# Two-layer diffusion backbone: modulation blocks of layer 2 moved to another stretch, FFN value groups regrouped, operand sums moved

## The chip, the cores and the metric

One core of a Trainium2 chip runs the whole program. The metric is the device time of one execution in microseconds; the time given for a kernel is the median of its runs.

## The reference

Two layers work on 512 latent tokens and 256 context tokens of width 1024. Each layer has a token mixer of four branches, merged by gates, and a SwiGLU FFN of hidden width 2816. Both are modulated: a row vector per token kind (`c` for latents, `c_ctx` for the context) is made by one dense product with `w_ada[l]` and cut into six parts, a shift, a scale and a residual gate for the mixer and the same three for the FFN.

```python
mod_x = silu_c @ w_ada[l] + b_ada[l]        # sh_m, sc_m, g_m, sh_f, sc_f, g_f
mod_c = silu_cc @ w_ada[l] + b_ada[l]
hx = modulate(rms_norm(x, norm_mix[l]), sh_m, sc_m)
...
x = x + g_m * mixer_stream(px, ...)         # gates * branches, summed, @ w_out
if not last:
    ctx = ctx + cg_m * mixer_stream(pc, ...)
    ctx = ctx + cg_f * swiglu(modulate(rms_norm(ctx, norm_ffn), csh_f, csc_f), w1, w3, w2)
x = x + g_f * swiglu(modulate(rms_norm(x, norm_ffn), sh_f, sc_f), w1, w3, w2)
return rms_norm(x, final_norm)

def swiglu(h, w1, w3, w2):
    return (silu(h @ w1) * (h @ w3)) @ w2
```

In layer 2 the context is needed for keys and values only, so there only the shift and scale of its mixer are needed: the second and third 2048 columns of `w_ada[1]` matter for the latent row alone.

## The kernel before, in words

Tokens lie along the free axis, channels along the partitions, 128 at a time. Every fp32 matrix product is made of three matmuls, with both operands split into a high and a low part (`mm3`, L526 to L528; `mm3u`, L610 to L612, in the mixer's dense part; `prod`, L1654 to L1659, in the FFN of layer 1). Weights are split on the way: SP issues the load (L231), ScalarE casts the high part `wh` (L221), VectorE subtracts it to get the low part `wl` (L223), with three raw buffers and four each for high and low parts; `Stream` does the same in the dense part (L560, L566, L573).

The layer loop starts at L622. A layer has the mixer, then the *dense stretch* of gates and branch projections, then `w_out` (L1570 and on) with its residual, the norm, and the FFN. `dense` (L1484) runs gate units. Each yield of a unit feeds the weight stream, and every second one (`AJ`) calls a step of the *modulation generator*, from the third unit on.

That generator is `ada_steps` (L112). It makes 2048 columns of `w_ada` (block b of 0, 1, 2) in four quarters of eight steps. A step has a load of 256 KB on SP (L120), and on VectorE, for each row, one multiply (L133) or multiply-add (L131) of 128x512. At the end of a quarter TensorE transposes the accumulator in four pieces (L145) and VectorE reduces them (L146). `live` says how many rows (token kinds) each block has. An `issue_after` makes all its VectorE work wait for the last low part of the norm issued before (`lastn`, L182). Block 0 has shift and scale of the mixer, block 1 the mixer's residual gate and the FFN's shift, block 2 the FFN's scale and its gate. For layer 1, blocks 1 and 2 are made in layer 1's dense stretch. For layer 2 all three are made during layer 1's FFN (L1583), through `ada_next`: `NAF` steps behind each pass of FFN blocks, `NAN` steps behind each weight load of a down projection.

The FFN of layer 1 has 22 blocks of 128 hidden channels (`groups`), each group first up (`ffn_up` or `ffn_pair`), then down through `w_ffn2` (loop at L1794), with the result added to the residual stream by `resid` (L1565). `ffn_up` (L1594) makes a block from its weights directly, for given token ranges: `oh` is 0 to 512 and 512 to 768, `halves` is 0 to 384 and 384 to 768. `ffn_pair` makes two blocks at once by `quad` (L1661), a Strassen-like scheme with seven products of half size. It needs sums of weights (made by POOL, split as above) and sums of activations T1 to T4, which `prepare` (L1611) makes once, by POOL, VectorE and ScalarE; T1 overwrites a part of `h`. In the first group the first four blocks (`NCV`) go by ranges, while `norm_range` (L184) of the second range runs: a step of it per block, with squares and statistics, POOL's power, the broadcast transposes (L202), and for each of eight chunks a product (L208), an affine and a cast on ScalarE (L178, L181) and the low part (L182). In the last group the down projection goes range by range, and the norm for layer 2 follows each range.

In layer 2 the FFN has no pairs, and deeper weight buffers of its own pool `gp` (three extra `wh` and `wl`, eight `ws`), which lie where the mixer's pools were. Before it, `mg`, the merged branches, is split (L1557, L1558).

The order of the instructions on each engine is planned ahead of the run: a planner goes through the program and gives each engine, of what it holds to be ready, what stands first in the program. So work that stands later fills gaps, and a stall at run time is not replanned.

Of the kernel before, what the change touches and what calls it, by code (L numbers as in the profile page):

```python
# [43 lines left out]
NAN = 5  # L44
NCV = 4
# [18 lines left out]
def block_kernel(ctx: ExitStack, tc: tile.TileContext, x, c, ctx_in, c_ctx, w_ada, b_ada, norm_mix, w_in,  # L64
# [557 lines left out]
    for l in range(DEPTH):  # L622
# [10 lines left out]
        with ExitStack() if l else first as st:  # L633
# [836 lines left out]
            if l == 0:  # L1470
                ab = []

                def three():
                    flat = sbank().rearrange("p a b -> p (a b)")
                    return [flat[:, i * 512:(i + 1) * 512] for i in range(3)]

                def abufs():
                    if not ab:
                        ab.extend(utile(512, "wada") for _ in range(5))
                    return ab[:2], ab[2:]  # L1480

                ada = [ada_steps(0, b, three, abufs) for b in (1, 2)]
# [21 lines left out]
        with ExitStack() as st:  # L1504
# [76 lines left out]
            if not last:  # L1581
                wb = [gp.tile([P, 512], F32, tag="wada", name="wada", bufs=4) for _ in range(4)]
                ada = [ada_steps(1, b, lambda: [pf.tile([P, 512], F32, tag="ada", name="pa")],  # L1583
                                 lambda: (wb[:2], wb[2:]), (2, 1, 1)) for b in range(3)]
# [26 lines left out]
            def prepare():  # L1611
                def flat(t):
                    return t.rearrange("p (k n) -> p k n", k=4)

                def blk(i, kb, half):
                    return h[:, i, 4 * kb:4 * kb + 4, HT * half:HT * (half + 1)]

                def put(dst, v):
                    nc.scalar.copy(dst[:, 0], v)
                    nc.vector.tensor_sub(dst[:, 1], v, dst[:, 0])  # L1620

                def scratch():
                    return gp.tile([P, 4, HT], F32, tag="ga", name="sc", bufs=6)

                t3, t2, t4 = [gp.tile([P, 2, 4, HT], F32R, tag="tb", name="tb", bufs=3) for _ in range(3)]
                v, u = scratch(), scratch()
                nc.gpsimd.tensor_sub(u, blk(1, 1, 1), blk(1, 0, 1))
                nc.vector.tensor_sub(v, blk(0, 1, 1), blk(0, 0, 1))
                nc.vector.tensor_add(v, v, u)
                put(t3, v)  # L1630
                v2 = scratch()
                nc.gpsimd.tensor_add(v2, v, blk(1, 0, 0))
                nc.vector.tensor_add(v2, v2, blk(0, 0, 0))
                put(t2, v2)
                u4 = scratch()
                nc.gpsimd.tensor_sub(u4, blk(1, 1, 0), v2)
                nc.vector.tensor_add(u4, u4, blk(0, 1, 0))
                put(t4, u4)
                nc.gpsimd.tensor_sub(v2, blk(1, 1, 1), v2)
                nc.vector.tensor_add(v2, v2, blk(0, 1, 1))  # L1640
                t1 = h[:, :, 0:4, HT:2 * HT]
                put(t1, v2)
                tops.update(T1=t1, T2=t2, T3=t3, T4=t4, B11=h[:, :, 0:4, 0:HT], B21=h[:, :, 4:8, 0:HT],
                            B22=h[:, :, 4:8, HT:2 * HT])

# [112 lines left out]
            if fast:  # L1758
                groups = [list(range(0, 6)), list(range(6, 12)), list(range(12, 18)), list(range(18, 22))]
            for gi, grp_ in enumerate(groups):  # L1760
# [6 lines left out]
                elif gi == 0:  # L1767
                    todo = [(grp_[:NCV], [r]) for r in oh]
                elif fast:
                    todo = []  # L1770
                for fs, rngs in todo:
# [8 lines left out]
                    if f:  # L1780
                        ada_next(NAF)
                if fast:
                    if gi == 0:
                        prepare()
                    for f in grp_[NCV if gi == 0 else 0::2]:
# [8 lines left out]
                for rngs in ([[r] for r in oh] if lastg else [halves]):  # L1794
                    for n in range(NC_):
# [3 lines left out]
                        ada_next(NAN)  # L1799
# [70 lines left out]
```

## Time and profile before

| | |
|---|---|
| median of 3 runs | 2665.15 us (2663.88 to 2666.01) |
| the profiled execution's own time | 2665.27 us |
| its span, first to last instruction | 2663.3 us |
| TensorE busy | 2548.0 us (96%), mean granted clock 0.985 |
| VectorE busy | 1852.1 us (70%) |
| ScalarE busy | 1171.7 us (44%) |
| GpSimd busy | 237.2 us (9%) |

PE is TensorE, DVE is VectorE, ACT is ScalarE, POOL is GpSimd, SP issues most loads. A matmul's busy time covers the whole time that it is in the pipeline, so matmuls overlap, and a busy share near 100% can hide a slow stream: the number of matmuls in a window tells more. A row of the groups reads: line, engine, operation, output<-inputs, shapes, count | busy us, mean ns of one | idle before, and what ended it.

### The profile page before, as it was taken

To read this page: it belongs to the slowest core of one execution; us is meant where nothing else is said; L and a number is where in the kernel's file an instruction comes from. 1 tells how busy PE (TensorE), PEld (TensorE's weight loads), DVE (VectorE), ACT (ScalarE), POOL (GpSimd) and SP (SyncE) were. 2 spreads that over 40 slices of the span, in tenths; PEclk is the share of its full clock that TensorE was granted. 3 is DMA by queue.
4 is the path that set the end of the run, shared out by engine and by line. 5 is a ranking of instruction groups with operands and counts; after the bars stand their busy time and mean duration, and the time that the engine had idled before them with its cause. 6 is when DMAs were issued, how large, how long until landed. Compare 5 with 4: busy or idle time off the path is not lost.

```text
span 2663.3 us, 38749 instructions
## 1 busy us (share of the span) xinstructions
PE 2548.0 (96%) x14435; PEld 2328.1 (87%) x14435; DVE 1852.1 (70%) x3205; ACT 1171.7 (44%) x2324; POOL 237.2 (9%) x255
## 2 busy tenths in 40 slices
PE   7999999999999998898999999999999999999998
PEld 5999889999999987898999978788888888988888
DVE  5967887786878668888675579887766635733335
ACT  5245555556422354323232354566665423722235
POOL 2000000000000011223030310100000000000000
PEclk9999999999999999999999999999999999999999
DMA  8211112222245354354442243111222235633333
GB/s 289 69 40 44 44 33 72 60 62 66 90 141 168 112 172 116 95 158 136 146 119 60 68 133 92 52 44 52 64 78 73 73 96 157 177 98 95 96 95 111
DMA packets 400800, 262.53 MB, mean 99 GB/s; under 512 B 15946, under 2 KB 368532, under 8 KB 400612
## 3 DMA queue, kind: packets, MB, share of 16 engines
q1 hardware_dynamic: 393332, 236.14, 30.0%
q0 software_dynamic: 7280, 23.93, 3.2%
q8 instruction: 113, 1.85, 0.3%
q14 instruction: 75, 0.61, 0.1%
HBM read 243.23 MB, written 8.91 MB: 95 GB/s over the span
## 4 chain that ended last, share of the span: by engine, by line
PE 80%; DVE 8%; issue 4%; DMA 4%; ACT 3%; SPq 0%; POOL 0%; DVEq 0%; POOLq 0%; ACTq 0%
PE pf L610 10%; PE pf L611 10%; PE pf L612 10%; PE pf L528 10%; PE pf L527 10%; PE pf L526 10%; PE pf L1658 8%; PE pS L907 3%; PE pT L936 2%; DMA wada<-in_w_ada_dram 2%; PE pv L1346 2%; PE pv L1435 1%; DVE wl L223 1%; DVE wada L131 1%; DMA ws<-in_w_in_dram 1%
## 5 line engine op out<-in xcount | busy, mean ns | idle before, releaser
L221 ACT CAST wh<-ws 128x512 fp32r<-128x512 f32 (+2 forms) x407 | 242.2, 600 | 531.1 <-PE pf L527 370.4
L610 PE MATMUL pf<-h,wh 128*128 128x384 f32 (+1 forms) x1280 | 459.4, 359 | 1.9 <-ACT tg L782 1.3
L612 PE MATMUL pf<-h,wl 128*128 128x384 f32 (+1 forms) x1280 | 448.7, 351 | 0.0
L611 PE MATMUL pf<-h,wh 128*128 128x384 f32 (+1 forms) x1280 | 447.8, 350 | 0.0
L223 DVE TENSOR_TENSOR wl<-ws,wh 128x512 fp32r<-128x512 f32 (+2 forms) x407 | 277.1, 686 | 186.9 <-ACT wh L221 183.0
L528 PE MATMUL pf<-h,wl 128*128 128x512 f32 (+2 forms) x784 | 279.1, 359 | 8.2 <-DVE wl L223 8.2
L526 PE MATMUL pf<-h,wh 128*128 128x512 f32 (+2 forms) x784 | 277.1, 360 | 8.8 <-ACT h L181 5.3
L527 PE MATMUL pf<-h,wh 128*128 128x512 f32 (+2 forms) x784 | 279.3, 359 | 1.0 <-DVE h L182 0.9
L566 ACT CAST wh<-ws 128x512 fp32r<-128x512 f32 x264 | 164.1, 623 | 235.3 <-PE pf L611 197.5
L610 PEld LDWEIGHTS pf<-h,wh 128*128 128x128 f32 x1280 | 241.6, 189 | 16.3 <-ACT tg L782 2.0
L611 PEld LDWEIGHTS pf<-h,wh 128*128 128x128 f32 x1280 | 241.8, 189 | 13.4 <-issue 0.6
L612 PEld LDWEIGHTS pf<-h,wl 128*128 128x128 f32 x1280 | 241.0, 188 | 13.3 <-issue 0.2
L573 DVE TENSOR_TENSOR wl<-ws,wh 128x512 fp32r<-128x512 f32 x264 | 181.1, 687 | 96.8 <-ACT wh L566 95.6
L704 DVE SCALAR_TENSOR_TENSOR ca<-ub,cols,ca 128x798 f32<-128x798 f32 (+1 forms) x240 | 215.3, 897 | 4.0
L131 DVE SCALAR_TENSOR_TENSOR wada<-wada,sil 128x512 f32<-128x512 f32 x224 | 183.6, 840 | 30.5 <-DMA wada<-in_w_ada_dram 28.9
L527 PE MATMUL pf<-g,wh 128*128 128x384 f32 (+2 forms) x584 | 197.4, 339 | 0.0
L528 PE MATMUL pf<-g,wl 128*128 128x384 f32 (+2 forms) x584 | 196.1, 339 | 0.0
L526 PE MATMUL pf<-g,wh 128*128 128x384 f32 (+2 forms) x584 | 195.8, 340 | 0.0
L526 PEld LDWEIGHTS pf<-h,wh 128*128 128x128 f32 x784 | 148.3, 192 | 31.5 <-ACT h L181 7.9
L528 PEld LDWEIGHTS pf<-h,wl 128*128 128x128 f32 x784 | 150.2, 192 | 29.4 <-DVE wl L223 10.0
L527 PEld LDWEIGHTS pf<-h,wh 128*128 128x128 f32 x784 | 150.1, 192 | 23.5 <-DVE h L182 4.2
L938 ACT CAST pt<-pT 128x512 fp32r<-128x512 f32 (+1 forms) x216 | 91.8, 471 | 153.9 <-PE pT L936 153.4
(385 smaller groups left out, 5127.7 us busy)
## 6 DMA issues: line engine op xcount, KB each, us to landing
ws<-in_w_in_dram SPq DMA_DIRECT2D x248, 256.0 KB, 2.9
ws<-in_w_ffn_dram SPq DMA_DIRECT2D x243, 256.0 KB, 2.9
wada<-in_w_ada_dram SPq DMA_DIRECT2D x160, 256.0 KB, 3.0
ws<-in_w_out_dram SPq DMA_DIRECT2D x58, 256.0 KB, 3.1
sq<-in_w_ffn_dram SPq DMA_DIRECT2D x45, 256.0 KB, 4.2
wada<-in_w_ada_dram SPq DMA_DIRECT2D x16, 512.0 KB, 6.8
khl<-khl POOLq DMA_DIRECT2D x40, 192.0 KB, 3.1
ws<-in_w_ffn_dram SPq DMA_DIRECT2D x24, 192.0 KB
```

The costliest lines, as they stand in the source:

```text
L131: nc.vector.scalar_tensor_tensor(accs[r], w, s, accs[r], op0=ALU.mult, op1=ALU.add)
L221: nc.scalar.copy(wh[:, :n], st[:, :n])
L223: lastv[0] = nc.vector.tensor_sub(wl[:, :n], st[:, :n], wh[:, :n]).ins
L526: nc.tensor.matmul(o, lhsT=wh, rhs=xh(k), start=(k == 0), stop=False)
L527: nc.tensor.matmul(o, lhsT=wh, rhs=xl(k), start=False, stop=False)
L528: nc.tensor.matmul(o, lhsT=wl, rhs=xh(k), start=False, stop=(k == n - 1))
L573: nc.vector.tensor_sub(wl, u.raw[i], u.wh[i])
L610: nc.tensor.matmul(o, lhsT=wh, rhs=xh(k), start=(k == 0), stop=False)
L611: nc.tensor.matmul(o, lhsT=wh, rhs=xl(k), start=False, stop=False)
L612: nc.tensor.matmul(o, lhsT=wl, rhs=xh(k), start=False, stop=(k == nk - 1))
L704: nc.vector.scalar_tensor_tensor(a, u, w, a, op0=ALU.mult, op1=ALU.add)
L1658: nc.tensor.matmul(o, lhsT=wt_, rhs=T[:, x_, k], start=(start and k == 0 and i == 0), stop=(stop and k == 3 and i == 2), skip_group_check= ...
```

## The change

Blocks 1 and 2 of layer 2's modulation are made in layer 2's own dense stretch, with one row each; block 0 stays in layer 1's FFN, but its steps come in down projections of the second group on. The groups of layer 1's FFN become 4, 6, 6, 6 in place of 6, 6, 6, 4. In the first group, blocks 0 and 1 go by ranges and blocks 2 and 3 by halves with one load; the pair (4, 5) goes to the second group, so there are still nine pairs. `prepare` becomes a generator of eight steps on half the columns each, one step per output block of the first down projection.

```diff
@@ -41,8 +41,7 @@
 NTS = (2, 2)
 AJ = 2
 NAF = 3
-NAN = 5
-NCV = 4
+NAN = 4
 NAQ = 0
 NSL = 4
 WB = (0, 3)
@@ -1467,7 +1466,7 @@
                 fill.flush()
             conv_split(3, 4)
             ada = []
-            if l == 0:
+            if True:
                 ab = []
 
                 def three():
@@ -1479,7 +1478,7 @@
                         ab.extend(utile(512, "wada") for _ in range(5))
                     return ab[:2], ab[2:]
 
-                ada = [ada_steps(0, b, three, abufs) for b in (1, 2)]
+                ada = [ada_steps(l, b, three, abufs, (1, 1, 1) if last else (2, 2, 2)) for b in (1, 2)]
 
             def dense(units, skip=0):
                 for i, u in enumerate(units):
@@ -1581,7 +1580,7 @@
             if not last:
                 wb = [gp.tile([P, 512], F32, tag="wada", name="wada", bufs=4) for _ in range(4)]
                 ada = [ada_steps(1, b, lambda: [pf.tile([P, 512], F32, tag="ada", name="pa")],
-                                 lambda: (wb[:2], wb[2:]), (2, 1, 1)) for b in range(3)]
+                                 lambda: (wb[:2], wb[2:])) for b in range(1)]
 
             def ada_next(n):
                 for _ in range(n):
@@ -1609,39 +1608,37 @@
             tops = {}
 
             def prepare():
-                def flat(t):
-                    return t.rearrange("p (k n) -> p k n", k=4)
-
-                def blk(i, kb, half):
-                    return h[:, i, 4 * kb:4 * kb + 4, HT * half:HT * (half + 1)]
-
-                def put(dst, v):
-                    nc.scalar.copy(dst[:, 0], v)
-                    nc.vector.tensor_sub(dst[:, 1], v, dst[:, 0])
-
-                def scratch():
-                    return gp.tile([P, 4, HT], F32, tag="ga", name="sc", bufs=6)
-
                 t3, t2, t4 = [gp.tile([P, 2, 4, HT], F32R, tag="tb", name="tb", bufs=3) for _ in range(3)]
-                v, u = scratch(), scratch()
-                nc.gpsimd.tensor_sub(u, blk(1, 1, 1), blk(1, 0, 1))
-                nc.vector.tensor_sub(v, blk(0, 1, 1), blk(0, 0, 1))
-                nc.vector.tensor_add(v, v, u)
-                put(t3, v)
-                v2 = scratch()
-                nc.gpsimd.tensor_add(v2, v, blk(1, 0, 0))
-                nc.vector.tensor_add(v2, v2, blk(0, 0, 0))
-                put(t2, v2)
-                u4 = scratch()
-                nc.gpsimd.tensor_sub(u4, blk(1, 1, 0), v2)
-                nc.vector.tensor_add(u4, u4, blk(0, 1, 0))
-                put(t4, u4)
-                nc.gpsimd.tensor_sub(v2, blk(1, 1, 1), v2)
-                nc.vector.tensor_add(v2, v2, blk(0, 1, 1))
                 t1 = h[:, :, 0:4, HT:2 * HT]
-                put(t1, v2)
                 tops.update(T1=t1, T2=t2, T3=t3, T4=t4, B11=h[:, :, 0:4, 0:HT], B21=h[:, :, 4:8, 0:HT],
                             B22=h[:, :, 4:8, HT:2 * HT])
+                for k in (0, 2):
+                    def blk(i, kb, half):
+                        return h[:, i, 4 * kb + k:4 * kb + k + 2, HT * half:HT * (half + 1)]
+
+                    def put(dst, v):
+                        nc.scalar.copy(dst[:, 0, k:k + 2], v)
+                        nc.vector.tensor_sub(dst[:, 1, k:k + 2], v, dst[:, 0, k:k + 2])
+
+                    u, v = [gp.tile([P, NTOK], F32, tag="ts", name="ts", bufs=2).rearrange("p (k n) -> p k n", k=2)
+                            for _ in range(2)]
+                    nc.gpsimd.tensor_sub(u, blk(1, 1, 1), blk(1, 0, 1))
+                    nc.vector.tensor_sub(v, blk(0, 1, 1), blk(0, 0, 1))
+                    nc.vector.tensor_add(v, v, u)
+                    put(t3, v)
+                    yield
+                    nc.gpsimd.tensor_add(u, v, blk(1, 0, 0))
+                    nc.vector.tensor_add(u, u, blk(0, 0, 0))
+                    put(t2, u)
+                    yield
+                    nc.gpsimd.tensor_sub(v, blk(1, 1, 0), u)
+                    nc.vector.tensor_add(v, v, blk(0, 1, 0))
+                    put(t4, v)
+                    yield
+                    nc.gpsimd.tensor_sub(u, blk(1, 1, 1), u)
+                    nc.vector.tensor_add(u, u, blk(0, 1, 1))
+                    put(t1, u)
+                    yield
 
             def sqtile(name):
                 sqn[0] += 1
@@ -1756,7 +1753,7 @@
 
             groups = [list(range(0, 8)), list(range(8, 15)), list(range(15, 22))]
             if fast:
-                groups = [list(range(0, 6)), list(range(6, 12)), list(range(12, 18)), list(range(18, 22))]
+                groups = [list(range(0, 4)), list(range(4, 10)), list(range(10, 16)), list(range(16, 22))]
             for gi, grp_ in enumerate(groups):
                 gt = []
                 for f in grp_:
@@ -1765,7 +1762,7 @@
                 if gi == 0 and last:
                     todo = [(grp_[:NSL], [r]) for r in oh] + todo[NSL:]
                 elif gi == 0:
-                    todo = [(grp_[:NCV], [r]) for r in oh]
+                    todo = [(grp_[:2], [r]) for r in oh] + todo[2:]
                 elif fast:
                     todo = []
                 for fs, rngs in todo:
@@ -1777,12 +1774,9 @@
                         ffn_up(f, gt[f - grp_[0]], rngs)
                         next(nr, None)
                     drain(nr)
-                    if f:
-                        ada_next(NAF)
-                if fast:
-                    if gi == 0:
-                        prepare()
-                    for f in grp_[NCV if gi == 0 else 0::2]:
+                prep = prepare() if fast and gi == 0 else iter(())
+                if fast and gi:
+                    for f in grp_[::2]:
                         ffn_pair(f, gt[f - grp_[0]], gt[f + 1 - grp_[0]])
                 lastg = gi == len(groups) - 1
                 if lastg:
@@ -1796,7 +1790,9 @@
                         if n in (1, 3, 5, 7):
                             next(fin, None)
                         ws = wload(w_ffn2[l], grp_[0] * P, n * P, len(grp_))
-                        ada_next(NAN)
+                        next(prep, None)
+                        if gi or not fast:
+                            ada_next(NAN)
                         for lo, hi in rngs:
                             pu = gbank()[:, :hi - lo]
                             mm3(pu, ws, lambda k: gt[k][:, 0, lo:hi], lambda k: gt[k][:, 1, lo:hi])
```

## Rows read from the trace of the kernel before

**Rows 1.** The page, the chain that ended last, by engine.

```profile
PE 80%; DVE 8%; issue 4%; DMA 4%; ACT 3%; SPq 0%; POOL 0%; DVEq 0%; POOLq 0%; ACTq 0%
```

**Rows 2.** Unbroken matmul streams, windows: us, busy (count) by engine, clock, DMA.

```profile
1440.00:1460.00 20.00, 20.00 (x116) 20.00 (x115) 9.07 (x20) 3.88 (x8) 0.00 (x0) 1.00 0.20 60
...
2240.00:2260.00 20.00, 20.00 (x171) 20.00 (x170) 11.84 (x22) 7.87 (x14) 0.00 (x0) 1.00 0.68 178
```

**Rows 3.** The same view, layer 1's FFN.

```profile
1034.50:1100.00 65.50, 48.34 (x268) 43.93 (x267) 63.52 (x71) 22.64 (x37) 20.77 (x7) 0.84 0.44 128
1160.00:1280.00 120.00, 107.36 (x585) 103.57 (x584) 101.99 (x152) 37.74 (x66) 41.01 (x27) 0.96 0.49 151
1280.00:1380.00 100.00, 96.29 (x540) 94.43 (x539) 71.76 (x120) 27.69 (x49) 17.89 (x12) 0.98 0.46 136
```

**Rows 4.** The same windows, records of L1658 (one) and of L145 (two) alone.

```profile
1034.50:1100.00 65.50, 16.27 (x66) 14.42 (x67) 0.84 0.44 128
...
1160.00:1280.00 120.00, 3.98 (x24) 2.97 (x24) 0.96 0.49 151
1280.00:1380.00 100.00, 2.40 (x16) 2.00 (x16) 0.98 0.46 136
```

**Rows 5.** TensorE's waits, 1160 to 1380 us.

```profile
PE pf L1658 <- DVE u L1692: 6.9, 3, 3.3
PE pf L1658 <- DVE wl L223: 5.0, 4, 2.2
```

**Rows 6.** VectorE's groups, 1034.5 to 1100 us: busy us, mean ns.

```profile
L131 DVE SCALAR_TENSOR_TENSOR wada<-wada,sil 128x512 f32<-128x512 f32 x22 | 24.9, 1148 | 1.2 <-DMA wada<-in_w_ada_dram 1.1
...
L1628 DVE TENSOR_TENSOR sc<-h 128x1536 f32<-128x1536 f32 x1 | 1.8, 1752 | 0.0
```

**Rows 7.** Timeline of POOL and of VectorE; columns: start us, us, instruction.

```profile
1060.19 3.46 POOL L1636 TENSOR_TENSOR sc<-h,sc 128x1536 f32<-128x1536 f32 x1 [7.86 <-DVE sc L1633]
...
1060.27 3.93 DVE L223 TENSOR_TENSOR wl<-ws,wh 128x512 fp32r<-128x512 f32 x1
```

**Rows 8.** Timeline of TensorE and VectorE around the second range's norm.

```profile
1012.66 0.38 PE L202 MATMUL pT<-ident,r 128*128 128x128 f32 x2
...
1025.25 0.42 DVE L182 TENSOR_TENSOR h<-hn,h 128x256 fp32r<-128x256 f32 x1
1025.59 4.13 DVE L133 TENSOR_SCALAR wada<-wada,sil 128x512 f32<-128x512 f32 x2
```

**Rows 9.** VectorE's groups, first down projection, 1110 to 1160 us.

```profile
L223 DVE TENSOR_TENSOR wl<-ws,wh 128x512 fp32r<-128x512 f32 x8 | 5.5, 689 | 0.7 <-ACT wh L221 0.7
L1565 DVE SCALAR_TENSOR_TENSOR xT<-pf,mod,xT 128x384 f32<-128x384 f32 x6 | 3.7, 612 | 4.9 <-PE pf L528 4.9
...
L1565 DVE SCALAR_TENSOR_TENSOR xT<-pf,mod,xT 128x256 f32<-128x256 f32 x6 | 2.8, 474 | 0.0
...
L1565 DVE SCALAR_TENSOR_TENSOR xT<-pf,mod,xT 128x128 f32<-128x128 f32 x6 | 2.1, 344 | 0.0
...
L1723 DVE TENSOR_TENSOR g<-ts,g 128x768 fp32r<-128x768 f32 x2 | 1.8, 954 | 0.9 <-ACT g L1722 0.9
```

**Rows 10.** Timeline of TensorE, first matmul of layer 2's projections.

```profile
1578.46 0.80 PE L526 MATMUL pf<-h,wh 128*128 128x512 f32 x1 [5.30 <-ACT h L181]
```

**Rows 11.** Layer 1's dense stretch: its window, VectorE's L131 in it, modulation reductions.

```profile
745.00:905.00 160.00, 160.00 (x940) 159.42 (x939) 127.51 (x217) 33.93 (x62) 0.00 (x0) 1.00 0.49 147
...
L131 DVE SCALAR_TENSOR_TENSOR wada<-wada,sil 128x512 f32<-128x512 f32 x96 | 69.0, 746 | 5.5 <-DMA wada<-in_w_ada_dram 4.3 <-DVE wada L131 0.4
...
L146 DVE TENSOR_REDUCE mod<-pS x8: 680/686/692, 829.3 to 892.3; 128x4 f32<-128x512 f32 x8
```

**Rows 12.** Window of layer 2's dense stretch.

```profile
2093.00:2225.00 132.00, 131.69 (x593) 108.05 (x591) 54.96 (x87) 39.01 (x69) 1.38 (x1) 1.00 0.30 86
```

**Rows 13.** Timeline of TensorE, start of layer 2's output projection.

```profile
2231.25 0.58 PE L526 MATMUL pf<-mg,wh 128*128 128x256 f32 x1 [6.21 <-ACT wh L221]
```

**Rows 14.** Layer 1's FFN, multiply-adds with one row, 1278 to 1293 us.

```profile
L131 DVE SCALAR_TENSOR_TENSOR wada<-wada,sil x7: 744/751/754, 1278.6 to 1290.5; 128x512 f32<-128x512 f32 x7
```

## What the change was predicted to do

> **What bounds the kernel now.** First the chain of waits: four fifths of it is TensorE, VectorE has 8%, ScalarE 3% [rows 1]. So the time is the matmuls, which the change leaves alone, plus the stretches in which TensorE does less than it can. What it can do is read from windows in which it never stops: 116 matmuls of 384 columns in 20 us, 0.1724 us each, and 171 of 256 columns, 0.117 us each [rows 2]. Next the windows of layer 1's FFN, with VectorE's column beside TensorE's [rows 3]; the records of pairs (L1658) and of modulation transposes (L145) give the shapes [rows 4].
>
> - 1034.5 to 1100 us (second-range pass of the first four blocks, the sums for the pairs, start of pair (4,5)): 66 records of 384 columns and 202 narrow ones need 66 x 0.1724 + 202 x 0.117 = 35.0 us; the window has 65.5, so 30.5 are lost. VectorE is busy 63.5 of 65.5, and the mean granted clock is 0.84, part of it at the 1.2 GHz level: that cost is inside the 30.5.
> - 1160 to 1280 us (second group's pairs): 561 x 0.1724 + 24 x 0.117 = 99.5; 20.5 lost, VectorE 102 of 120.
> - 1280 to 1380 us: 524 x 0.1724 + 16 x 0.117 = 92.2; 7.8 lost, VectorE 72 of 100.
>
> Together 58.8 us. The waits say who is late: matmuls of pairs wait for VectorE's sums (L1692, 6.9 us) and low weight parts (L223, 5.0 us) [rows 5]. What crowds VectorE is the modulation of layer 2: its multiply-adds (L131) take 22 slots in the first window, of 1.148 us on average [rows 6]; the same instruction takes 0.746 undisturbed [rows 11].
>
> **The change, part by part.** Sums are made against the profiled execution, 2665.3 us (span 2663.3 and 2 around it); it lies 0.1 us from the median. A measurement can tell about 0.2%, 5.3 us, from no change.
>
> *What goes from layer 1's FFN.* Modulation blocks b=1 and b=2 leave (64 multiply steps with one row each, 64 loads on SP's queue, 8 x 4 transposes); b=0 stays with 64 steps (two rows) and is placed in the down projections of the later groups alone. The four wide preparation steps leave the crowded window. I remove the whole 58.8 us and charge the new stretches one by one. What is late next is then the norm of the second range.
>
> *(a) The norm of the second range.* Its broadcast (L202) runs at 1012.66, right behind the second block of the first pass (the code takes one step of the norm per block), and the last low part of h starts at 1025.25, taking 0.42 us [rows 8]: 13.0 us, covered today by blocks 2 and 3. After the change the first pass holds two blocks, so TensorE has nothing wide left. Only block 0's 48 narrow matmuls of the second pass (48 x 0.117 = 5.6 us) can be done chunk by chunk meanwhile; later weights wait for the four weight buffers. 13.0 - 5.6: **+7.4** (0 if the norm is taken earlier, 11 if little interleaves).
>
> *(b) Second pass and blocks 2, 3.* VectorE has some 9 us of gating and low weight parts against the last 5.6 us of narrow matmuls, then wide work: **+4** (0 to 8).
>
> *(c) First down projection, now with the preparation.* TensorE: 8 x 2 x 12 x 0.1724 = 33 us. VectorE: the sums. A 1536-wide one took 1.75 us [rows 6], a 768-wide subtraction 0.95 [rows 9]: 18 half-size ones x 0.95 = 17; 8 low weight parts x 0.69 = 5.5; residuals 8 x (0.612 + 0.474 + 0.344) = 11.4 [rows 9]. That is 34. To this comes blocking: while POOL worked 3.46 us on the sum at 1060.19, a low part (L223) issued at 1060.27 took 3.93 us instead of 0.69 [rows 7]; four such pairs stand in the trace, about 3.2 us each, 12.6 in all. Halves halve each POOL instruction and double their number, so again 12.6: 46 against 33. But about 11 us of the preparation is ready while blocks 2 and 3 still fill TensorE. **+3** (0 to 15).
> The Trainium skill (SBUF — State Buffer, Who interferes with whom and SBUF: two separate sides) calls the port pair of the two engines an exclusive lock that the first holds for its whole instruction. The row of 3.93 us agrees. By the rule alone, every POOL instruction here would block VectorE; that is rival C.
>
> *(d) First pairs and the rest of b=0.* Half of the modulation stays in the FFN, now 64 steps x 0.746 = 48 us spread over two down projections and their neighbours; those have room (7.8 lost even in the third window with it). **+5** (0 to 20, the upper end being the 20.5 of the second window). So the FFN gives -58.8 + 19.4 = -39.4.
>
> *(e) Boundary to layer 2.* The last group has six blocks instead of four, so each range pass is 8 x 18 matmuls of 256 columns (16.8 us) instead of 8 x 12 (11.2). The norm that makes TensorE idle 5.3 us before 1578.46 [rows 10] gets 5.6 us more cover. It also gets 16 more loads, casts and low parts of 256 columns in front of it. **-3.5** (-5.6 to +2). The eight loads saved in the first group offset those on SP's queue.
>
> *(f) Layer 2's dense stretch.* 64 steps and loads come in. Layer 1's dense stretch carries twice the steps: 160 us of TensorE in a 160 us window with VectorE at 127.5 [rows 11]. Layer 2's has VectorE at 55 of 132 us, TensorE at 131.7 [rows 12]; with 64 x 0.746 = 48 more it stays under. **+1.5** (0 to 4). Loads: DMA share 0.30 there against 0.49 in layer 1's, so SP's queue has room.
>
> *(g) The tail of it.* In 14 units of 7 yields, a step every second yield, 42 steps are placed in the dense stretch; b=1 takes 35, b=2 gets 7, and 28 (26 multiplies) stand behind it in the program. The five buffers lie where layer 2's FFN has high-part weight buffers, so w_out's first weights wait for the end of it. Layer 1 makes a quarter with two rows in about (892.3 - 829.3)/3 = 21 us [rows 11]. With one row and two buffers in the FFN the loads gave one step per 2.0 us (six intervals in 11.9) [rows 14]; three buffers, as here, should lie between that and 0.75: I take 1.5. Eight of these and about 6 us for transposes that wait for a matmul group to end: 18 us a quarter, 144 for eight. If, as in layer 1, steps run ahead of their place, they end 144 us behind 2093, at 2237. Today w_out starts at 2231.25 after 6.2 us idle [rows 13]; two of its first columns have other buffers and can go first. **+4** (0 to 15).
>
> Sum: -39.4 - 3.5 + 1.5 + 4 = -37.4: **2628 us**.
>
> **The rivals.**
>
> *A, slower: the tail stays in its place.* The planner leaves the last 26 steps behind the dense stretch. Nothing covers them: 26 x 2.0 + about 4 = 56 us, in place of the 6.6 us of today's gap: +50 instead of +4, at the start of w_out: 2628 + 46 = **2674**. It decides, that is, the time comes out over 2670.5, once the tail passes 46 us. For it: a new chain per quarter (one accumulator) and transposes that the planner puts at group ends. Against: steps ran ahead of their place in layer 1, and VectorE has 77 idle us of 132. 0.11.
>
> *B: the FFN gives half.* The release of the modulation (behind the last low part of the second-range norm) is unchanged, so b=0's steps may be pulled into the second pass and first pairs as now: its first step (L133) starts at 1025.59, as the norm's last low part ends [rows 8]. Half of 39.4 is 19.7 lost: **2648**. For it: the same planner. Against: b=0 stands behind the preparation now. 0.17.
>
> *C: first down projection bound by VectorE.* No preparation is taken ahead and all POOL work blocks: (46 - 33) = 13 and the second pass's 3 stay, less the +3 counted: **2641**. For it: the blocked low part [rows 7]. Against: small steps fit into gaps. 0.10.
>
> *D: B with a tail of about 20 us:* 2648 + 16 = 2664, no change. 0.05.
>
> **How the numbers follow.** The forecast has 0.57, its own range 2612 to 2640: the middle of the bounds of (a) to (g), not all at one end (every bound at its best would be 2665.3 - 58.8 - 5.6 = 2601). Range 2612 to 2660 takes in C and B, and leaves out A, D and 0.04 below 2612: 0.20. Faster by over 0.2%: 0.57 + 0.10 + 0.17 = 0.84; within it 0.05; slower 0.11.
>
> **What would show it.** Right: in the pairs of the second group near 116 matmuls per 20 us and a granted clock of 1.00; TensorE idle some 7 us before the first narrow pass of the FFN; eight POOL sums of 768 inside the first down projection; idle before layer 2's first matmul under 3 us; eight reductions (L146) in layer 2 from about 2110 to 2240 less the gain, and no idle over 12 us before w_out. Wrong: VectorE over 90% in the pair windows again (B); TensorE idle over 40 us before w_out with L131 running (A); TensorE waiting for weights all through the first down projection (C). A second-range norm longer than 13 us, or blocks 2 and 3 starved of low parts, would make (a) and (b) too small.

## The result, and the profile after

The changed kernel takes 2631.82 us (2631.12 to 2635.12, four runs) against 2664.52 us before (four runs): a ratio of 0.988, 95% interval 0.9863 to 0.9897. Forecast was 2628 us, between 2612 and 2660. The profiled execution's span fell from 2663.3 to 2630.6 us, by 32.7. Line numbers of the changed kernel are lower by one up to `ada_next` (L525 to L527 for L526 to L528, L130 for L131, L222 for L223) and by three in `prod` (L1655).

The chain of waits, in the page of the changed kernel, against [rows 1]: VectorE's share is down from 8% to 6%, TensorE's up by three points.

```profile
PE 83%; DVE 6%; ACT 4%; issue 3%; DMA 3%; POOL 0%; SPq 0%; DVEq 0%; POOLq 0%; ACTq 0%
```

The windows of layer 1's FFN, where [rows 3] stood. From the top: the second range's norm and narrow pass; blocks 2 and 3 and the first down projection; the pairs of the second group; its down projection and the next pairs.

```profile
1012.30:1040.00 27.70, 21.23 (x120) 19.64 (x119) 25.93 (x40) 16.93 (x33) 8.51 (x4) 0.82 0.36 105
1040.00:1103.70 63.70, 63.70 (x367) 63.70 (x366) 47.70 (x71) 17.04 (x28) 10.53 (x6) 1.00 0.29 88
1103.70:1205.00 101.30, 92.24 (x515) 88.57 (x514) 92.23 (x135) 35.85 (x63) 31.78 (x20) 0.98 0.37 108
1205.00:1380.00 175.00, 174.93 (x1001) 174.48 (x1001) 100.15 (x175) 54.33 (x96) 37.03 (x27) 1.00 0.25 71
```

By the sum that the prediction used: the first window holds 19 matmuls of 384 columns, 3 of 512 (0.22 us each, as in the dense window below) and 98 narrow ones, 15.4 us of 27.7, so 12.3 are lost. The second needs 367 x 0.1724 = 63.3 of 63.7. The third needs 491 x 0.1724 + 24 x 0.117 = 87.5 of 101.3: 13.8 lost. The fourth 993 x 0.1724 + 8 x 0.117 = 172.1 of 175: 2.9. Together 29.4 us where 58.8 were: 29.4 gained, 39.4 were forecast.

Two matmuls tell the first window's story, in the timeline of TensorE:

```profile
1015.19 0.69 PE L525 MATMUL pf<-h,wh 128*128 128x256 f32 x2 [2.15 <-ACT h L180]
...
1033.01 0.58 PE L527 MATMUL pf<-h,wl 128*128 128x256 f32 x1 [3.59 <-DVE wl L222]
```

The first waits 2.15 us for the high part that the norm makes, the second 3.59 us for a low weight part. Behind each wait the granted clock was at the lower of its two levels (1.2 of 2.4 GHz) for a while, 0.52 and 0.50 in these windows:

```profile
1015.20:1018.50 3.30, 3.30 (x14) 3.09 (x15) 2.77 (x9) 3.17 (x7) 0.00 (x0) 0.52 0.27 79
1033.00:1039.20 6.20, 6.20 (x23) 6.20 (x24) 6.20 (x9) 2.23 (x5) 3.37 (x2) 0.50 0.63 192
```

14 and 23 matmuls stand there. By the rates above they need 1.6 and 3.4 us, so some 4.5 of the 12.3 us are the clock (an estimate). What lowered it isn't shown: in run e3 below TensorE waits the same 2.15 us, and the clock behind it is 1.00. What VectorE does during the second wait stands in its timeline, under a sum of POOL:

```profile
1026.64 1.96 POOL L1630 TENSOR_TENSOR ts<-ts,h 128x768 f32<-128x768 f32 x1 [2.70 <-DVE ts L1627]
...
1026.82 2.47 DVE L132 TENSOR_SCALAR wada<-wada,sil 128x512 f32<-128x512 f32 x2
1029.21 0.74 DVE L130 SCALAR_TENSOR_TENSOR wada<-wada,sil 128x512 f32<-128x512 f32 x1
1029.87 0.95 DVE L1621 TENSOR_TENSOR tb<-ts,tb 128x768 fp32r<-128x768 f32 x1
1030.74 0.74 DVE L130 SCALAR_TENSOR_TENSOR wada<-wada,sil 128x512 f32<-128x512 f32 x1
1031.40 0.95 DVE L1631 TENSOR_TENSOR ts<-ts,h 128x768 f32<-128x768 f32 x1
1032.27 1.28 DVE L222 TENSOR_TENSOR wl<-ws,wh 128x512 fp32r<-128x512 f32 x2
```

Modulation steps of block 0 (L132, L130) and sums of the preparation (L1621, L1631) stand ahead of the low parts (L222, 1032.27). Both had been written for later places in the program; the planner pulled both ahead. The two multiplies (L132) take 2.47 us beside the POOL sum, where such a multiply takes 0.61 us on average in the pairs, so the blocking by POOL is over 1 us of the wait (an estimate). In the pairs, too, the steps were pulled ahead: 41 of block 0's multiply-adds run there, and matmuls wait for low parts and sums, as in [rows 5, 6] (VectorE's groups from 1103.7 to 1205 us; then TensorE's waits from 1012 to 1210 us):

```profile
L130 DVE SCALAR_TENSOR_TENSOR wada<-wada,sil 128x512 f32<-128x512 f32 x41 | 34.3, 869 | 1.5 <-DMA wada<-in_w_ada_dram 1.4
...
PE pf L1655 <- DVE wl L222: 4.5, 4, 1.9
...
PE pf L1655 <- DVE u L1681: 1.8, 1, 1.8
```

The first down projection lost nothing. In its timeline a POOL sum still stretches a VectorE instruction (2.20 us for a low part of 384 columns, which takes 0.56 in run e4), and its window has 194 matmuls in 33.7 us, the full rate:

```profile
1071.83 2.23 POOL L1630 TENSOR_TENSOR ts<-ts,h 128x768 f32<-128x768 f32 x1 [24.74 <-DVE ts L1627]
...
1071.67 0.69 DVE L222 TENSOR_TENSOR wl<-ws,wh 128x512 fp32r<-128x512 f32 x1
1072.27 2.20 DVE L1605 TENSOR_TENSOR g<-tf,g 128x384 fp32r<-128x384 f32 x1
...
1070.00:1103.70 33.70, 33.70 (x194) 33.70 (x193) 26.39 (x41) 8.63 (x13) 7.20 (x4) 1.00 0.22 64
```

At the boundary to layer 2, the 5.30 us of [rows 10] are gone; the first matmul comes at once, and small waits of 0.2 to 0.4 us follow.

```profile
1542.54 0.39 PE L525 MATMUL pf<-h,wh 128*128 128x512 f32 x1
...
1546.06 0.50 PE L525 MATMUL pf<-h,wh 128*128 128x512 f32 x1 [0.42 <-ACT h L180]
```

Layer 2's dense stretch, in place of [rows 12, 13]: its window, the reductions of blocks 1 and 2, and TensorE's last waits ahead of w_out.

```profile
2060.00:2190.00 130.00, 130.00 (x599) 107.36 (x598) 94.89 (x150) 37.04 (x65) 1.39 (x1) 1.00 0.66 202
...
L145 DVE TENSOR_REDUCE mod<-pS x8: 683/684/686, 2081.7 to 2194.8; 128x4 f32<-128x512 f32 x8
...
2193.60 1.12 PE L144 MATMUL pS<-ident,wada 128*128 128x128 f32 x4 [2.72 <-DVE wada L130]
2199.55 0.58 PE L525 MATMUL pf<-mg,wh 128*128 128x256 f32 x1 [4.84 <-ACT wh L220]
```

VectorE does 94.9 us of work in 130, and TensorE keeps its 599 matmuls. The eight reductions end at 2194.8, with the dense stretch. w_out now waits 2.72 + 4.84 = 7.56 us in place of 6.21. The reason stands in VectorE's queue:

```profile
2192.79 0.75 DVE L130 SCALAR_TENSOR_TENSOR wada<-wada,sil 128x512 f32<-128x512 f32 x1 [1.05 <-DMA wada<-in_w_ada_dram]
2193.46 0.68 DVE L788 SCALAR_TENSOR_TENSOR tg<-tg,pf 128x512 f32<-128x512 f32 x1
2194.18 0.69 DVE L789 TENSOR_TENSOR macc<-macc,tg 128x512 f32<-128x512 f32 x1
```

The last multiply (2192.79) had waited for its load; the last gate product (L788, 2193.46) stands behind it, so the last merge (L789) and then the casts of `mg` and of the weights start late.

### The profile page after: what moved, and what is told of

The parts are those of the page before. It is cut to its first block, busy times and chain, and to the rows that moved or that the text cites. A ratio compares the mean times of both kernels' runs of the same rounds, so it can differ in the third digit from the quotient of the medians.

```text
span 2630.6 us, 38775 instructions
## 1 busy us (share of the span) xinstructions
PE 2533.5 (96%) x14435; PEld 2319.5 (88%) x14435; DVE 1845.4 (70%) x3214; ACT 1170.8 (45%) x2328; POOL 237.6 (9%) x259
## 4 chain that ended last, share of the span: by engine, by line
PE 83%; DVE 6%; ACT 4%; issue 3%; DMA 3%; POOL 0%; SPq 0%; DVEq 0%; POOLq 0%; ACTq 0%
PE pf L527 11%; PE pf L525 11%; PE pf L526 11%; PE pf L609 10%; PE pf L610 10%; PE pf L611 10%; PE pf L1655 8%; PE pS L906 3%; PE pT L935 2%; PE pv L1345 2%; PE pv L1434 1%; DMA wada<-in_w_ada_dram 1%; DVE wada L130 1%; ACT e L925 1%; DVE wl L222 1%
## 5 line engine op out<-in xcount | busy, mean ns | idle before, releaser
L222 DVE TENSOR_TENSOR wl<-ws,wh 128x512 fp32r<-128x512 f32 (+2 forms) x407 | 276.6, 685 | 203.9 <-ACT wh L220 200.2
L527 PE MATMUL pf<-h,wl 128*128 128x512 f32 (+2 forms) x784 | 277.2, 357 | 3.7 <-DVE wl L222 3.6
L526 PE MATMUL pf<-h,wh 128*128 128x512 f32 (+2 forms) x784 | 278.1, 358 | 1.6 <-DVE h L181 1.5
L525 PE MATMUL pf<-h,wh 128*128 128x512 f32 (+2 forms) x784 | 274.0, 358 | 4.5 <-ACT h L180 2.8
L527 PE MATMUL pf<-g,wl 128*128 128x384 f32 (+2 forms) x584 | 197.5, 340 | 2.4 <-DVE wl L222 2.4
L525 PE MATMUL pf<-g,wh 128*128 128x384 f32 (+2 forms) x584 | 196.8, 340 | 0.9 <-ACT wh L220 0.9
L526 PE MATMUL pf<-g,wh 128*128 128x384 f32 (+2 forms) x584 | 197.5, 339 | 0.0
L130 DVE SCALAR_TENSOR_TENSOR wada<-wada,sil 128x512 f32<-128x512 f32 x224 | 170.8, 783 | 23.8 <-DMA wada<-in_w_ada_dram 21.7
L527 PEld LDWEIGHTS pf<-h,wl 128*128 128x128 f32 x784 | 149.4, 191 | 22.9 <-DVE wl L222 4.6
L525 PEld LDWEIGHTS pf<-h,wh 128*128 128x128 f32 x784 | 146.8, 191 | 25.0 <-ACT h L180 5.0
L526 PEld LDWEIGHTS pf<-h,wh 128*128 128x128 f32 x784 | 149.3, 191 | 21.6 <-DVE h L181 3.6
```

Source lines behind the costliest of these rows:

```text
L130: nc.vector.scalar_tensor_tensor(accs[r], w, s, accs[r], op0=ALU.mult, op1=ALU.add)
L222: lastv[0] = nc.vector.tensor_sub(wl[:, :n], st[:, :n], wh[:, :n]).ins
L525: nc.tensor.matmul(o, lhsT=wh, rhs=xh(k), start=(k == 0), stop=False)
L526: nc.tensor.matmul(o, lhsT=wh, rhs=xl(k), start=False, stop=False)
L527: nc.tensor.matmul(o, lhsT=wl, rhs=xh(k), start=False, stop=(k == n - 1))
```

## The experiments

All ratios below are to the kernel before, run on the same chip; the changed kernel is 2631.8 us.

### Which half of the change gains what

Run e1: the kernel before with the move of blocks 1 and 2 alone.

```diff
-            if l == 0:
+            if True:
                 ab = []
...
-                ada = [ada_steps(0, b, three, abufs) for b in (1, 2)]
+                ada = [ada_steps(l, b, three, abufs, (1, 1, 1) if last else (2, 2, 2)) for b in (1, 2)]
...
-                                 lambda: (wb[:2], wb[2:]), (2, 1, 1)) for b in range(3)]
+                                 lambda: (wb[:2], wb[2:])) for b in range(1)]
```

> The kernel before with only blocks 1 and 2 of layer 2's modulation moved to layer 2's dense stretch; groups, preparation and the places of block 0's steps as before. Theory (the FFN loses where modulation steps meet pairs on VectorE): block 0's 64 steps end near 1105 us, before the second group's pairs, so the 28 us lost between 1160 and 1380 us go, the 30 us of 1034 to 1100 stay, layer 2 costs 2: about 2638 us. Rival (the gain is that of the regrouping and of the moved preparation): under 8 us gained, 2657 or more.

Measured: 2645.0 us, ratio 0.9925 (0.9911 to 0.994): 19 us gained. The same windows as [rows 3]:

```profile
1034.50:1100.00 65.50, 46.61 (x268) 42.24 (x267) 63.69 (x71) 22.75 (x37) 20.75 (x7) 0.87 0.44 130
1160.00:1280.00 120.00, 117.77 (x671) 116.45 (x671) 85.44 (x132) 42.36 (x74) 38.54 (x27) 1.00 0.28 83
1280.00:1380.00 100.00, 99.93 (x572) 99.62 (x571) 56.37 (x91) 33.92 (x60) 27.58 (x20) 1.00 0.24 68
```

The first window keeps 268 matmuls, the very number of before, and the third is at its full rate (572). The second has 671 instead of 585; with the 32 more of the third that is 118 x 0.1724 = 20 us. The 4 to 5 us that the second still misses I put down to block 0, whose last transposes came at 1181, not at 1105. So the theory holds in kind, 7 us short of its number, with block 0 slower than I had put it.

Run e2: the changed kernel with blocks 1 and 2 made in layer 1's FFN again.

```diff
-            if True:
+            if l == 0:
                 ab = []
...
-                ada = [ada_steps(l, b, three, abufs, (1, 1, 1) if last else (2, 2, 2)) for b in (1, 2)]
+                ada = [ada_steps(0, b, three, abufs) for b in (1, 2)]
...
-                                 lambda: (wb[:2], wb[2:])) for b in range(1)]
+                                 lambda: (wb[:2], wb[2:]), (2, 1, 1)) for b in range(3)]
...
-NAN = 4
+NAN = 5
```

> The changed kernel with blocks 1 and 2 made in layer 1's FFN again (five steps per weight load, as before); groups of 4, 6, 6, 6 and the preparation in the first down projection stay. Theory: the first window's 30 us fall to some 16, the boundary gains 3, but 128 steps crowd the pairs of the second and third group for 20 to 28 us and more: about 2650 us. Rival (regrouping and preparation are the gain): 2638 us or less.

Measured: 2650.1 us, 0.9941 (0.9924 to 0.9957): 14 us gained. Its windows, shifted by 1 to 2 us:

```profile
1014.00:1042.00 28.00, 21.41 (x127) 19.75 (x126) 25.55 (x40) 16.63 (x33) 8.14 (x4) 0.88 0.35 104
1042.00:1104.00 62.00, 62.00 (x356) 62.00 (x356) 48.07 (x71) 17.16 (x30) 10.93 (x6) 1.00 0.29 87
1104.00:1206.00 102.00, 93.16 (x526) 89.23 (x525) 93.83 (x138) 35.85 (x63) 31.79 (x20) 1.00 0.38 113
1206.00:1380.00 174.00, 164.68 (x914) 159.72 (x913) 133.38 (x221) 50.57 (x90) 39.73 (x27) 0.98 0.50 150
```

The first three windows are as in the changed kernel, and the fourth loses what the moved blocks cost (914 matmuls instead of 1001). 19 + 14 = 33 us: the two halves add up to the whole, 32.7.

### What the FFN still loses

Run e3: block 0's VectorE work queued behind the pairs of its group, and spread over three down projections.

```diff
                     nc.scalar.copy(g[:, 0], t)
-                    nc.vector.tensor_sub(g[:, 1], t, g[:, 0])
+                    lastn[0] = nc.vector.tensor_sub(g[:, 1], t, g[:, 0]).ins
...
-NAN = 4
+NAN = 2
```

> The changed kernel; block 0's VectorE work is queued behind the last low part of the pairs of its group, and two steps per weight load stand in each of the three later down projections instead of four. Theory (block 0's steps, pulled ahead of their place, are what the first pairs lose to): of 17.7 us lost between 1103 and 1205 us some 14 go, and part of the 13 of the second range's pass: 2614 to 2619 us, over 114 matmuls per 20 us in those pairs. Rival (pairs lose to their own sums, low parts and POOL's sums): at most 4 us gained, 2628 or more.

Measured: 2615.4 us, 0.9817 (0.9803 to 0.9832). The first and third window of the changed kernel:

```profile
1012.30:1040.00 27.70, 22.27 (x144) 19.93 (x143) 25.84 (x38) 17.77 (x35) 8.95 (x5) 1.00 0.29 83
...
1103.70:1205.00 101.30, 101.23 (x579) 100.92 (x578) 66.77 (x103) 39.01 (x68) 25.13 (x19) 1.00 0.25 71
```

579 matmuls in place of 515 in the pairs, at a granted clock of 1.00: 579 x 0.1724 is 99.8 of the 101.3 us, and the pairs' own sums, low parts and POOL's sums never were too much. The first window gets 144 in place of 120; by the same sum it loses 8.2 us instead of 12.3, now at a clock of 1.00. This is 16 us, nearly the whole loss of the pairs and a part of that of the narrow pass. The run has two edits, the hold and the spreading of the steps (`NAN`), and no run splits them.

Run f3 puts the same hold on e1's kernel, with the old groups and the wide preparation.

```diff
-                    nc.vector.tensor_sub(g[:, 1], t, g[:, 0])
+                    lastn[0] = nc.vector.tensor_sub(g[:, 1], t, g[:, 0]).ins
...
-NAF = 3
-NAN = 5
+NAF = 0
+NAN = 2
```

> The kernel with the move of blocks 1 and 2 only (groups and preparation as before), with block 0's steps held behind the pairs of each group, two per weight load and none behind the range passes. Theory (of 63.5 us of VectorE in the first window, the steps are some 30; without them its loss falls from 31 to 10 to 18 us): 2622 to 2632 us. Rival (wide sums and POOL's sums alone bound the narrow passes): 2637 us or more.

Measured: 2624.1 us, 0.9851 (0.9834 to 0.9868): 21 us under e1.

```profile
1034.50:1100.00 65.50, 58.31 (x363) 55.11 (x362) 54.66 (x58) 29.91 (x51) 19.48 (x9) 0.95 0.30 87
```

363 matmuls where 268 were, with more pairs among them. Of 192 narrow, 146 of 384 and 25 of 512 columns these need 53.1 us, so 12.4 are lost where e1 lost 30. So most of the first window's loss before was the modulation too. What remains may be the wide preparation, but no run holds that one back.

### The preparation and the cover of the norm

Run e4: VectorE's part of the preparation queued behind the last low part of the first four blocks.

```diff
-                    nc.vector.tensor_sub(g[:, 1, lo:hi], t, g[:, 0, lo:hi])
+                    lastg_[0] = nc.vector.tensor_sub(g[:, 1, lo:hi], t, g[:, 0, lo:hi]).ins
...
-                        next(prep, None)
+                        with tc.issue_after(lastg_[0]):
+                            next(prep, None)
```

> The changed kernel; VectorE's part of the preparation is queued behind the last low part of the first four blocks, so that none of it is taken ahead of the first down projection. Theory (the first down projection lost nothing because half of the preparation, 1022 to 1047 us, was taken ahead of it): the 3.8 us stall in the second range's pass goes, but the down projection gets 46 us of VectorE work against 33 of TensorE and loses 8 to 13: 2635 to 2641 us. Rival (small steps fit between the low parts, the preparation never was a bound there): 2627 to 2630 us.

Measured: 2630.7 us, 0.9873 (0.9858 to 0.9888): within its spread of the changed kernel. The window of the norm, those of the down projection and of the pairs, the stretch of the preparation, and the one matmul that waits at its end:

```profile
1012.30:1040.00 27.70, 24.34 (x153) 22.76 (x152) 23.47 (x44) 15.66 (x32) 1.85 (x1) 0.94 0.46 136
...
1070.00:1103.70 33.70, 33.70 (x194) 33.66 (x193) 32.82 (x41) 9.67 (x14) 15.35 (x8) 1.00 0.14 40
1103.70:1205.00 101.30, 90.46 (x500) 86.11 (x499) 97.81 (x143) 36.38 (x64) 32.35 (x20) 0.98 0.38 112
...
1067.40:1106.10 38.70, 36.83 (x212) 36.56 (x210) 37.55 (x49) 11.88 (x18) 15.54 (x8) 1.00 0.15 43
...
1106.05 0.99 PE L1656 MATMUL pf<-h,wh 128*128 128x384 f32 x4 [1.87 <-ACT wh L221]
```

All of VectorE's part of the preparation is beside the down projection now. In the window of 33.7 us VectorE is busy 32.8, and TensorE has the same 194 matmuls. But the preparation doesn't end with that window: it runs from 1067.4 to 1106.1 us, with VectorE busy 37.6 of the 38.7, and at its end the first pair waits 1.87 us for its weights. The theory falls all the same: the price is about 38 us of work rather than 46, and a wait of 2 us rather than 8 to 13. The first window gains 33 matmuls, 6 us by the sum used above, and the pairs give a part of that back (500 where the changed kernel has 515).

Run e5 holds both (the diffs of e3 and e4 together).

> Block 0's steps held as in the run that held them, and the preparation held to the first down projection as in the run that held it. Theory (the second range's pass loses to early preparation beside VectorE's low parts; the first down projection has room for all of it): 3 to 6 us under the kernel that holds block 0 alone, 2609 to 2612 us. Rival (VectorE was busy 32.8 of 33.7 us in that down projection, so with it full the pairs behind it start late): no gain, 2615 to 2619.

Measured: 2616.8 us, 0.9827 (0.9813 to 0.984): no gain over e3. The window of the norm, that of the down projection, and the one wait at its end:

```profile
1012.30:1040.00 27.70, 25.22 (x163) 23.32 (x162) 16.35 (x32) 14.90 (x31) 1.85 (x1) 1.00 0.34 97
...
1070.00:1103.70 33.70, 32.02 (x183) 31.69 (x181) 33.45 (x44) 10.12 (x16) 13.71 (x7) 1.00 0.14 40
...
1104.31 1.01 PE L1656 MATMUL pf<-h,wh 128*128 128x384 f32 x4 [2.29 <-ACT wh L221]
```

The first pair's weights come 2.29 us late: the rival. It is e4's wait, 1.7 us earlier, so that it falls into the window and leaves it 183 matmuls. The first window shows the norm's own loss, without either kind of side work on VectorE and with the clock at 1.00: 55 matmuls of 384 columns, 10 of 512 and 98 narrow ones need 23.1 us of 27.7, so 4.6 are lost.

Run e6 adds a third block by ranges to e5; run f1 adds it to e3, and run f2 to the changed kernel:

```diff
-                    todo = [(grp_[:2], [r]) for r in oh] + todo[2:]
+                    todo = [(grp_[:3], [r]) for r in oh] + todo[3:]
```

> The kernel that holds both, with three blocks by ranges in the first group and one by halves. Theory (what is left at the second range is its norm without cover): 48 more wide matmuls, some 11 us, lie beside the 13 us of the norm, and the wait of 2.4 us before the first narrow matmul and the stalls behind it go: 3 to 5 us under the kernel that holds both. Rival (narrow passes are bound by the low parts, so a third block by ranges, with its weights loaded and split twice, gives back what the cover gains): within 2 us of that kernel or over it.

> The changed kernel with block 0's steps held and three blocks by ranges; the preparation is free to run early. Theory (cover of the norm and held steps add up; holding the preparation cost 2.5 us in the first pairs): 2606 to 2609 us. Rival (early preparation meets the low parts of three narrow blocks and stalls them): 2612 us or more.

> The changed kernel with three blocks by ranges and nothing else. Theory (the norm's missing cover is a loss of its own): the 2.4 us before the first narrow matmul and the slow start go, 3 to 6 us: 2626 to 2629 us. Rival (with block 0's steps and the preparation beside it, a longer narrow pass loses as much again, as in the kernel before): 2630 to 2636 us.

Measured: e6 2610.3 us, 0.9801 (0.9787 to 0.9814); f1 2615.5 us, 0.9817 (0.9803 to 0.9832); f2 2634.7 us, 0.9892 (0.9873 to 0.991). The same 47.7 us in the changed kernel, f2, f1 and e6, in this order:

```profile
1012.30:1060.00 47.70, 41.23 (x236) 39.64 (x235) 42.73 (x63) 21.72 (x42) 11.84 (x5) 0.89 0.39 117
```

```profile
1012.30:1060.00 47.70, 38.93 (x232) 34.72 (x231) 43.50 (x64) 22.86 (x45) 12.01 (x5) 0.96 0.42 123
```

```profile
1012.30:1060.00 47.70, 43.10 (x268) 39.44 (x267) 36.43 (x54) 24.80 (x48) 9.83 (x5) 1.00 0.35 100
```

```profile
1012.30:1060.00 47.70, 47.70 (x306) 45.82 (x306) 28.79 (x53) 24.81 (x50) 1.86 (x1) 1.00 0.40 117
```

The third block covers the norm in all three: no matmul waits for it any more. But it also lengthens the narrow pass, and there the low parts meet what the planner pulls ahead: with modulation and preparation (f2) VectorE is busy 43.5 us and the cover is worth nothing; with the preparation alone (f1) 36.4 us, and again nothing; with neither (e6) 28.8 us, and TensorE never stops (47.7 busy of 47.7). The longest single waits in f1 and f2 (2.09 and 2.34 us) are for a weight's high part, whose cast had waited for its load. So the cover paid, 6.5 us, where both were held, and not with block 0 alone held or with neither; with the preparation alone held it wasn't run. The rival came true in f1 and f2, the theory in e6, with more than its 3 to 5 us. e6 is the fastest version here, 21.5 us under the changed kernel.

### The tail in layer 2

Run e7: a block with one row takes its two accumulators in turn.

```diff
+        def ac(r, q):
+            return accs[r if nr == 2 else q % 2]
...
-                        nc.vector.scalar_tensor_tensor(accs[r], w, s, accs[r], op0=ALU.mult, op1=ALU.add)
+                        nc.vector.scalar_tensor_tensor(ac(r, q), w, s, ac(r, q), op0=ALU.mult, op1=ALU.add)
```

> The changed kernel; a block with one row takes its two accumulators in turn, a quarter each, so that a quarter's first multiply no longer waits for the transposes of the quarter before. Theory (a quarter in layer 2's dense stretch takes 16.95 us because its transposes wait for the end of a gate unit, and the last quarter's multiplies hold VectorE's queue at the end of that stretch): quarters of 13 to 16 us, the last reduction 10 us or more before the dense stretch ends, about 2 us less: 2629 to 2631 us. Rival (the loads set the pace): the last reduction stays within 4 us of its place, no change.

Measured: 2639.2 us, 0.9908 (0.9894 to 0.9921): 7 us slower than the changed kernel. The dense window; TensorE's wait for gate products; and VectorE's queue at one of them:

```profile
2060.00:2190.00 130.00, 123.42 (x564) 99.88 (x564) 94.60 (x153) 35.27 (x61) 1.39 (x1) 1.00 0.67 204
...
PE pf L613 <- DVE tg L792: 4.8, 4, 1.8
...
2112.47 0.48 DVE L136 TENSOR_SCALAR wada<-wada,sil 128x512 f32<-128x512 f32 x1 [1.38 <-DMA wada<-in_w_ada_dram]
2112.87 0.68 DVE L792 SCALAR_TENSOR_TENSOR tg<-tg,pf 128x512 f32<-128x512 f32 x1
```

The steps do run faster: the last reduction starts at 2166.6, 28 us earlier. But the window has 564 matmuls instead of 599. A multiply that waits for its load (1.38 us, 2112.47) has the gate product (L792 here) behind it in VectorE's queue, and TensorE waits 1.48 us for that; the three other waits for a product have such a multiply just ahead too. In the changed kernel the transposes, taken at the end of a gate unit, hold the steps to two units a quarter. That this keeps them out of the way is my reading; no run varies it alone. My theory had the pace right and the effect with the wrong sign.

Run e8 leaves out 48 of the 64 multiplies and loads of these blocks, so the modulation of layer 2 lacks most of its terms.

```diff
-        chunks = [(q, k) for q in range(4) for k in range(NC_)]
+        chunks = [(q, k) for q in range(4) for k in ((0, NC_ - 1) if l and b else range(NC_))]
```

> The changed kernel with blocks 1 and 2 of layer 2's modulation cut to their first and last chunk in each quarter: 48 of the 64 multiplies and loads are left out, so the modulation is not that of the reference. Theory (they lie beside dense matmuls and cost 2 to 5 us in all): 2627 to 2630 us. Rival (the tail behind the dense stretch is what keeps the kernel at 2632 rather than lower, as in the forecast's slower rival in small): 2622 us or less.

Measured: 2632.8 us, 0.9884 (0.987 to 0.9897), the time of the changed kernel.

```profile
2060.00:2190.00 130.00, 130.00 (x600) 107.26 (x599) 66.18 (x111) 35.65 (x61) 1.55 (x1) 1.00 0.37 112
...
PE pf L525 <- ACT wh L220: 6.2, 1, 6.2
```

600 matmuls against 599, and 6.2 us ahead of w_out against 7.56. So the 48 steps cost TensorE some 1.4 us by these waits, too little for the medians to show. VectorE's 29 us less of work are worth nothing there, and neither expectation came true.

## Why the prediction was right

The mechanism was right in the main, and the sum came out 4 us low. One term, (d), was 12 us too small; (c), (f) and (g) together were 7 us too large. So part of the nearness is luck.

- **The loss in the FFN and its cause** (58.8 us of crowding by the modulation): right. e1, e3 and f3 each take steps away, and the matmuls come back.
- **(a) and (b), the second range: +7.4 and +4 forecast, 12.3 measured.** The size was right, the parts weren't. The norm's own loss is 4.6 us (e5), not 7.4, and TensorE was idle 2.15 us before the narrow pass where I had named 7 as a sign. The other 7.7 come with early preparation and block 0's steps, which I had put under rival B, and with the lower clock: holding the one takes 6 us away (e4), holding the other 4 (e3).
- **(c), the first down projection: +3 forecast, 0.4 measured.** Half of the preparation was taken ahead as forecast, but earlier than beside blocks 2 and 3: from 1022 us, in the narrow pass, where it cost time. The price of 46 us was too high: e4 has it all there in about 38. Rival C is out. The blocked instructions are real (2.20 us beside POOL's 2.23), and delay nothing in this window. The Trainium skill (SBUF — State Buffer, Who interferes with whom) has the later one fully blocked; those two rows agree, and the window's 194 matmuls show that this block cost no time here.
- **(d), the first pairs: +5 forecast, 13.8 and 2.9 measured.** This is the step that was mis-sized. I trusted that the steps would stand in the down projections, where the program has them, and left their being pulled ahead to rival B. They were pulled ahead: the reductions of block 0 came from 1108.8 to 1224.9, through all pairs of the second group. These pairs ran at 102 matmuls per 20 us instead of 116, with VectorE busy 91%, which is the sign that I had named for rival B. It was half true: 10 us (39.4 less 29.4) of the 19.7 that it would have cost.
- **(e), the boundary: -3.5 forecast.** The 5.30 us idle became waits of 0.2 to 0.4 us behind the first matmul and 1.2 us inside the passes, and the clock behind the old wait (0.52 for 4 us) is 1.00; right in size as far as the rows show it.
- **(f), the dense stretch: +1.5 forecast, nothing measured** (599 matmuls, 600 with a quarter of the steps).
- **(g), the tail: +4 forecast, 1.4 measured.** Quarters of 16.9 us (18 forecast) and steps ahead of their place: right, and rival A is out. The place was wrong: the wait is VectorE's queue ahead of the last gate product, not a weight buffer of w_out. One figure of rival A was mis-added: 46 us is what the tail would have to add, the tail itself would have to pass 53.

The pieces: 29.4 in the FFN, some 3 at the boundary, less 1.4 at w_out make 31 of the 32.7 us. The rest I didn't trace.

## What to carry to other kernels

Where a planner fills gaps with whatever is ready, the place of side work in the program is only a wish: a thing moved out of a crowded stretch comes back to it unless something holds it. Look in the new trace for where it ran, and hold it behind the last instruction of the crowded stretch; here that hold, with the steps spread wider, gave 16 us, and another change (the third block) paid where both kinds of side work were held. Count matmuls per window before calling an engine too full, and look behind the window's end: VectorE at 97% cost one wait of 2 us in one place, and at 73% in another the kernel lost 7 us.

## What was not expected of the hardware

VectorE took its queue in order in these traces, so side work was dangerous for what it waited for rather than for what it took. In e7 VectorE did about the same work in the dense window as in the changed kernel (94.6 and 94.9 us), and TensorE lost 35 matmuls: ahead of each of the four gate products that it waited for stood a multiply that had waited 0.6 to 1.4 us for its load. In the changed kernel multiplies waited for loads as well (12.6 us in this window, 18.7 in e7), but TensorE waited for no gate product there.

And POOL seems to be held up as well as holding up: its 768-wide sums took 1.84 us at 1076.88 and 2.23 us at 1071.83, where a VectorE low part had begun 0.16 us before, while the VectorE instruction issued 0.4 us later took 2.20.
